# A decoder block on one core: vector work of the latent attention in pieces between products, four GpSimd operations moved to VectorE, stores of x pinned

## The chip, the cores and the metric

The kernel runs on one core of a Trainium2 chip. The metric is the device time of one execution in microseconds (us); of several runs the median counts. The engines of the core are named as in the profile: PE (TensorE, matrix products), DVE (VectorE), ACT (ScalarE), POOL (GpSimd) and SP (SyncE, which here issues nearly all the DMAs). Each engine works through its own queue of instructions in order, and waits for the other engines by semaphores.

## What is computed

Two decoder blocks for 512 tokens of width 1024, all in fp32. The first has four mixers side by side on one projection, then a feed-forward layer. The second has a gated linear recurrence beside a windowed attention, then attention to a memory of 256 tokens, then a convolutional feed-forward layer. Cut to what the change touches:

```
h = rms_norm(x, norm1_w);  cols = split_cols(h @ w_in, IN_SIZES)
y_a = short_conv_mixer(a_b, a_c, a_u, conv_w, conv_b)      # v = a_c * a_u;  a_b * (conv(v) + conv_b)
y_b = nsa_mixer(...)                                       # compressed + selected + windowed attention
y_c = mla_mixer(m_cq, m_ckv, m_kr, ...)                    # latent attention, below
y_d = stick_breaking_mixer(...)
x = x + grouped_rms_norm([y_a, y_b, y_c, y_d]) @ w_out;    x = x + relu(rms_norm(x) @ w1)**2 @ w2

def mla_mixer(c_q, c_kv, k_rope, ...):
    q = rms_norm(c_q) @ wq_b;  kv = rms_norm(c_kv) @ wkv_b       # 4 heads
    q = [q_nope, rope(q_rope)];  k = [k_nope, rope(k_rope)]
    o = causal_attention(rms_norm(q), rms_norm(k), v)

# second block
o = gla(q, 1 - f, log f, v) forward + backward              # 4 heads, 128 wide
y = gate * (rms_norm(o) * silu(g)) @ w_rec + gate * window_attention(...) @ w_att
mem_n = rms_norm(mem);  x = x + softmax((rms_norm(x) @ w_q) @ k_mem) @ v_mem @ w_o
```

## The kernel before

Tokens are cut into four tiles of 128. Every fp32 product is made of three passes: the left and the right operand are each split into a high and a low part (`Hkh`, `Hkl` for the normed input, `whi`, `wlo` for a weight), and PE multiplies high by high (L183), low by high (L184) and high by low (L185). A weight goes by a DMA of SP into `wraw`; ACT writes `whi` from it (L258) and DVE writes `wlo` (L259).

There is no written order of instructions over the whole program. The code is made of generators: a main line calls for attention heads step by step, and a side queue `fq` holds generators of projections. `fill(n)` takes n steps from the side queue, so that the products of projections stand on PE between the small products of an attention, during whose softmax on DVE and ACT PE would otherwise be idle. `drain()` runs what is left of the queue. A scheduler then puts the instructions of each engine into an order, roughly the order of the code, but it may move an instruction ahead of another where nothing forbids it.

In the first block (`side2`, in the function that runs the four mixers) the order is: the projection of the latent attention with `ncv` as its result; eight stores of x to `xs` (L674), from which x is read back later; `mla_stats`, which sums squares on ACT, takes a reciprocal root and scales `ncv` by it; `conv`, the projection of the convolution; the transposes and projections of the latent attention; `mla_rope`, which rotates, sums squares, takes a reciprocal root and scales again; `conv_gate`, the projection of the convolution's gate. `conv` and `conv_gate` yield in the middle of their products, the two others ran at one go. While this stands in the side queue, the heads of the sparse attention (NSA) are on the main line: for each unit of them the logits `L` are made by L889 and L890, DVE masks them and takes their maximum (L827, tiles `sba` and `sbam`), ACT makes the exponential (L828), PE transposes (L833, `pT`), ACT or DVE copy the transposed tile (`sbe`, L837 or L839), and PE multiplies by the values (L844).

`rsqrt_mean` makes a reciprocal root in one of two ways: for twelve or more columns by Ln and Exp on ACT with one step of Newton's method on DVE, for fewer by a power on POOL (L226). `token_rs` calls it with the sum of squares of each token, which L426 makes from `nacc`.

In the second block the recurrence runs over levels (`gla_head`): the product of level 0 needs a sum `gym` that POOL makes (L1549), its result is `lv` (L1555), and each further level needs products of DVE. After each level the main line takes steps of the side queue, which holds the projections of the next heads, of the gate and of `qkv`. The memory's norm (`token_rs` at L1741) stands between products of the cross-attention; its result reaches PE as `pt` (L439).

Of the kernel before, what the change touches and what calls it, by code (L numbers as in the profile page):

```python
# [148 lines left out]
class Kern:  # L149
# [50 lines left out]

    def rsqrt_mean(self, pool, out, ss, inv_n, tag):

        nc = self.nc
        n = 1
        for d in ss.shape[1:]:
            n *= d
        t = self.T(pool, [P] + list(ss.shape[1:]), F32, tag + "t")
        p = ss.shape[0]
        nc.vector.tensor_scalar(t[:p], ss, inv_n, EPS, op0=OP.mult, op1=OP.add)
        if n >= 12:  # L210

            u = self.T(pool, [P] + list(ss.shape[1:]), F32, tag + "u")[:p]
            t = t[:p]
            nc.scalar.activation(u, t, AF.Ln)
            nc.scalar.activation(out, u, AF.Exp, scale=-0.5)
            nc.vector.tensor_mul(u, out, out)
            nc.vector.tensor_mul(u, u, t)
            nc.vector.tensor_scalar(u, u, -0.5, 1.5, op0=OP.mult, op1=OP.add)
            nc.vector.tensor_mul(out, out, u)
            return  # L220
        e = self.mhalf[:p, :n]
        if len(ss.shape) == 3:
            e = e.rearrange("p (a b) -> p a b", b=ss.shape[2])
        elif len(ss.shape) == 4:
            e = e.rearrange("p (a b c) -> p a b c", b=ss.shape[2], c=ss.shape[3])
        nc.gpsimd.tensor_tensor(out, t[:p], e, op=OP.pow)  # L226
# [137 lines left out]
    def weave(a, b, n):  # L364

        for _ in a:
            yield
            for _ in range(n):
                next(b, None)
                yield  # L370

    def drain(self):
        self.fill(1 << 30)
# [45 lines left out]

    def token_rs(self, acc, N, inv_n, tag="o"):  # L420

# [5 lines left out]
        rs = self.T(self.sp, [P, nt], F32, "rs", 4)  # L427
        self.rsqrt_mean(self.sp, rs, stv[:, :, 0], inv_n, "rs")
        return rs
# [121 lines left out]
    def mixers1(self):  # L551
# [41 lines left out]
        with tc.tile_pool(name="mx", bufs=1) as mp:  # L593
# [69 lines left out]
            def side2():  # L663
# [8 lines left out]
                st["g"] = gN.rearrange("p t (h b) -> p t b h", b=3)  # L672
                for k in range(8):
                    nc.sync.dma_start(xs[:, k, :], self.x[k])  # L674
                self.mla_stats(mp, ncv)
                yield from self.conv(mp, nm, w)
                self.group_out(ySB, 3, "pT")
                cq = self.mla_trans(mp, ncv)
                yield
                yield from self.mla_proj(mp, ncv, cq, st)  # L680
                self.mla_rope(mp, ncv, st["mla"])
                yield from self.conv_gate(nm, w, st)
                norm = self.conv_norm(st["acc"])
# [267 lines left out]
    def conv(self, mp, nm, w):  # L951
# [3 lines left out]
        def ev_cu(c, b):  # L955
# [6 lines left out]
            nc.vector.tensor_mul(t, b, nm.R)  # L962
            nc.gpsimd.tensor_mul(v[c], t, v[c])
            cw = self.vec(f"cw{c}")
# [7 lines left out]
    def conv_gate(self, nm, w, out):  # L972
# [3 lines left out]
        def ev_b(c, b):  # L976
            y = self.yT[c]
            t = self.T(self.sp, [P, S], F32, "nsq", 2)
            nc.vector.tensor_mul(t, b, nm.R)
            nc.gpsimd.tensor_mul(y, y, t)  # L980
            self.dbg(f"yA{c}", y)
            if c == 0:
                nc.scalar.activation(acc, y, AF.Square)
            else:
                sq = self.T(self.sp, [P, S], F32, "nsq", 2)
                nc.scalar.activation(sq, y, AF.Square)
                nc.gpsimd.tensor_add(acc, acc, sq)
        yield from self.tproj_g(nm.H, w, [(0, 256)], ev_b)
# [255 lines left out]
    def mla_stats(self, mp, ncv):  # L1244
        nc = self.nc
        ss = self.T(mp, [P, NT, 2], F32, "mss", 1)
        for t in range(NT):
            nc.scalar.activation(self.junk(mp)[:, :192], ncv[:, t, :192], AF.Square, accum_out=ss[:, t, 0:1])
            nc.scalar.activation(self.junk(mp)[:, :128], ncv[:, t, 192:320], AF.Square, accum_out=ss[:, t, 1:2])
        nc.vector.tensor_scalar(ss[:, :, 0:1], ss[:, :, 0:1], 128.0 / 192.0, None, op0=OP.mult)  # L1250
        rr = self.T(mp, [P, NT, 2], F32, "mrr", 1)
        self.rsqrt_mean(mp, rr, ss, 1.0 / 128, "mrr")
        for t in range(NT):
            nc.vector.tensor_scalar(ncv[:, t, 0:192], ncv[:, t, 0:192], rr[:, t, 0:1], None, op0=OP.mult)
            nc.vector.tensor_scalar(ncv[:, t, 192:320], ncv[:, t, 192:320], rr[:, t, 1:2], None, op0=OP.mult)

    def mla_trans(self, mp, ncv):
# [38 lines left out]
    def mla_rope(self, mp, ncv, m):  # L1296
# [11 lines left out]
        for t in range(NT):  # L1308
            rope(qN[t][:, :, 64:96], t, 4)
            kr = ncv[:, t, 320:352].unsqueeze(1)  # L1310
            rope(kr, t, 1)
            nc.gpsimd.tensor_copy(kN[t][:, :, 64:96], kr.to_broadcast([P, 4, 32]))
        ss2 = self.T(mp, [P, 2, NT, 4], F32, "mss2", 1)
        for a, x in enumerate((qN, kN)):
            for t in range(NT):
                sq2 = self.T(mp, [P, S], F32, "mla_p", 3)[:, :384].rearrange("p (h d) -> p h d", d=96)
                nc.scalar.activation(sq2, x[t], AF.Square)
                nc.vector.tensor_reduce(ss2[:, a, t], sq2, axis=AX.X, op=OP.add)
        rr2 = self.T(mp, [P, 2, NT, 4], F32, "mrr2", 1)
        self.rsqrt_mean(mp, rr2, ss2, 1.0 / 96, "mrr2")  # L1320
        for a, x in enumerate((qN, kN)):
            for t in range(NT):
                nc.vector.tensor_mul(x[t], x[t], rr2[:, a, t].unsqueeze(2).to_broadcast([P, 4, 96]))

    def mla_head(self, h, prep):
# [71 lines left out]
    def mixers2(self):  # L1397
# [3 lines left out]
        with tc.tile_pool(name="b2", bufs=1) as bp:  # L1401
# [11 lines left out]
            with tc.tile_pool(name="gla", bufs=1) as gp:  # L1413
# [37 lines left out]
                for h in range(4):  # L1451
                    while st["n"] <= h:
                        self.fill(1)
                    if h == 0:
                        self.fill(5)
                    for lv, _ in enumerate(self.gla_head(gp, h, st, v)):
# [257 lines left out]
    def memory(self):  # L1714
# [4 lines left out]
        with tc.tile_pool(name="mem", bufs=1) as kp:  # L1719
# [3 lines left out]
            def prep():  # L1723
# [16 lines left out]
                yield  # L1740
                mn.rs = self.token_rs(mn.acc, 256, 1.0 / D, "pt")  # L1741
                yield
# [199 lines left out]
```

## Time and profile before

| | |
|---|---|
| time, median of 3 runs | 1625.76 us (1625.58 to 1626.16) |
| the profiled execution's own time | 1626.29 us |
| its span, from the first to the last instruction | 1624.6 us, mean granted clock 0.995 |
| PE busy | 1591.5 us, 98% of the span |
| DVE, ACT, POOL busy | 921.0, 667.0, 174.9 us (57%, 41%, 11%) |
| the chain that ended last | PE 90%, DVE 4%, ACT 2% |

The span is the stretch that the profile covers; what lies around it, 1.7 us, belongs to the time but not to the trace. Busy shares of the engines overlap: the chain's line says which engine's work, wait by wait, ended last.

### The profile page before, as it was taken

What the parts mean: (1) busy time and instruction counts of PE and PEld (TensorE: products, weight loads), DVE (VectorE), ACT (ScalarE), POOL (GpSimd) and SP (SyncE); (2) the same over time, 40 slices, a digit from 0 to 9 for tenths busy, and PEclk for the clock granted to TensorE, in tenths of its full rate; (3) what the DMA queues carried; (4) which work ended last, traced back from release to release, by engine and by line L of the source; (5) the groups of instructions that cost most, each with busy time, mean ns of one, the idle gap of its engine ahead of it and who ended that gap; (6) DMA issues with size and microseconds to landing.
All of it is one profiled execution on the core that took longest, in us unless ns stands there. A gap on an engine that the chain in (4) does not pass through costs nothing.

```text
span 1624.6 us, 20813 instructions
## 1 busy us (share of the span) xinstructions
PE 1591.5 (98%) x8049; PEld 1341.8 (83%) x8049; DVE 921.0 (57%) x1503; ACT 667.0 (41%) x1172; POOL 174.9 (11%) x185
## 2 busy tenths in 40 slices
PE   8999999999999999999999999999999999999998
PEld 6798888788888888878888788888988888888886
DVE  6666885644223434475766565664667556526662
ACT  5675554544123423334333354353544233222332
POOL 0121110200000001121110000330002111001110
PEclk9999999999999999999999999999999999999999
DMA  7242131232322223221222211323332333232331
GB/s 225 67 126 85 33 117 40 66 102 92 101 94 98 97 94 100 88 89 55 73 72 78 65 40 59 115 96 118 126 98 84 99 98 97 94 101 91 101 120 52
DMA packets 108118, 148.15 MB, mean 91 GB/s; under 512 B 7887, under 2 KB 58868, under 8 KB 108020
## 3 DMA queue, kind: packets, MB, share of 16 engines
q1 hardware_dynamic: 107876, 146.72, 28.3%
q8 instruction: 63, 1.03, 0.3%
q14 instruction: 35, 0.29, 0.1%
q10 hardware_dynamic: 144, 0.11, 0.0%
HBM read 142.31 MB, written 4.20 MB: 90 GB/s over the span
## 4 chain that ended last, share of the span: by engine, by line
PE 90%; DVE 4%; ACT 2%; issue 1%; POOL 1%; DMA 1%; SPq 0%; POOLq 0%; DVEq 0%; ACTq 0%
PE mm L183 25%; PE mm L185 25%; PE mm L184 25%; PE o L844 2%; PE lv L1570 2%; PE pT L833 1%; PE o L1613 1%; DVE wlo L259 1%; ACT whi L258 1%; PE L L889 1%; DMA wraw<-w_in_dram 1%; DMA wraw<-w_down_dram 1%; PE o L183 0%; PE o L185 0%; PE L L890 0%
## 5 line engine op out<-in xcount | busy, mean ns | idle before, releaser
L259 DVE TENSOR_TENSOR wlo<-wraw,whi 128x1024 fp32r<-128x1024 f32 (+4 forms) x268 | 319.5, 1194 | 439.2 <-ACT whi L258 434.5
L258 ACT ACTIVATE whi<-wraw 128x1024 fp32r<-128x1024 f32 (+4 forms) x268 | 270.4, 1010 | 536.9 <-PE mm L184 470.2
L417 POOL TENSOR_TENSOR nacc<-nacc,nsq 128x512 f32<-128x512 f32 x24 | 37.3, 1553 | 508.7 <-ACT nsq L415 507.6
L1866 POOL TENSOR_TENSOR fz<-fz,fu 128x512 f32<-128x512 f32 x22 | 37.4, 1698 | 269.6 <-ACT fz L1865 269.6
L461 DVE TENSOR_TENSOR x<-mm,x 128x512 f32<-128x512 f32 x72 | 48.9, 687 | 19.1 <-PE mm L185 18.8
L183 PE MATMUL mm<-H4h,whi 128*128 128x512 f32 x147 | 59.3, 404 | 0.0
L183 PE MATMUL mm<-H0h,whi 128*128 128x512 f32 x139 | 55.8, 402 | 2.9 <-ACT whi L258 2.9
L183 PE MATMUL mm<-H6h,whi 128*128 128x512 f32 x147 | 58.1, 399 | 0.4 <-ACT H6h L194 0.4
L183 PE MATMUL mm<-H7h,whi 128*128 128x512 f32 x147 | 58.3, 397 | 0.0
L185 PE MATMUL mm<-H4h,wlo 128*128 128x512 f32 x147 | 57.6, 392 | 0.7 <-DVE wlo L259 0.7
L183 PE MATMUL mm<-H5h,whi 128*128 128x512 f32 x147 | 58.1, 395 | 0.0
L185 PE MATMUL mm<-H6h,wlo 128*128 128x512 f32 x147 | 57.7, 393 | 0.0
L185 PE MATMUL mm<-H5h,wlo 128*128 128x512 f32 x147 | 57.7, 393 | 0.0
L184 PE MATMUL mm<-H6l,whi 128*128 128x512 f32 x147 | 57.7, 393 | 0.0
L184 PE MATMUL mm<-H5l,whi 128*128 128x512 f32 x147 | 57.4, 391 | 0.0
L184 PE MATMUL mm<-H4l,whi 128*128 128x512 f32 x147 | 57.4, 391 | 0.0
L185 PE MATMUL mm<-H7h,wlo 128*128 128x512 f32 x147 | 57.4, 390 | 0.0
L184 PE MATMUL mm<-H7l,whi 128*128 128x512 f32 x147 | 57.3, 390 | 0.0
L185 PE MATMUL mm<-H2h,wlo 128*128 128x512 f32 x139 | 54.5, 392 | 1.1 <-DVE wlo L259 1.1
L183 PE MATMUL mm<-H3h,whi 128*128 128x512 f32 x139 | 55.4, 399 | 0.0
L183 PE MATMUL mm<-H2h,whi 128*128 128x512 f32 x139 | 55.2, 397 | 0.0
L183 PE MATMUL mm<-H1h,whi 128*128 128x512 f32 x139 | 54.9, 395 | 0.0
(1264 smaller groups left out, 4340.1 us busy)
## 6 DMA issues: line engine op xcount, KB each, us to landing
wraw<-ffn_w_dram SPq DMA_DIRECT2D x64, 512.0 KB, 3.6
wraw<-w_up_dram SPq DMA_DIRECT2D x88, 256.0 KB, 2.8
wraw<-w_in_dram SPq DMA_DIRECT2D x36, 512.0 KB, 3.4
wraw<-w_down_dram SPq DMA_DIRECT2D x22, 512.0 KB, 3.6
wraw<-w_mem_kv_dram SPq DMA_DIRECT2D x16, 512.0 KB, 3.7
wraw<-w_in_dram SPq DMA_DIRECT2D x52, 128.0 KB, 2.3
wraw<-w_in_dram SPq DMA_DIRECT2D x20, 256.0 KB, 2.8
wraw<-cmp_w_dram SPq DMA_DIRECT2D x8, 512.0 KB, 4.0
```

Source lines behind the costliest of these rows:

```text
L183: mm(out, a.hi, b.hi, start=start, stop=False, skip_group_check=skip)
L184: mm(out, a.hi, b.lo, start=False, stop=False, skip_group_check=skip)
L185: mm(out, a.lo, b.hi, start=False, stop=stop, skip_group_check=skip)
L258: nc.scalar.activation(hi, raw, AF.Copy)
L259: nc.vector.tensor_sub(lo, raw, hi.bitcast(F32))
L417: eng.tensor_add(nm.acc, nm.acc, sq[:, :nm.N])
L461: self.nc.vector.tensor_add(self.x[k], b, self.x[k])
L833: nc.tensor.transpose(b[:, t * P:(t + 1) * P], st["p"][:, t * P:(t + 1) * P], self.ident)
L844: nc.tensor.matmul(o(), st["pT"][:, t * P:(t + 1) * P], v(t), start=(t == 0), stop=(t == nt - 1))
L889: self.nc.tensor.matmul(out, q[h][:, qs], k.hi[:, ks], start=True, stop=False)
L1570: nc.tensor.matmul(b[:, t * P:(t + 1) * P], ym[:, t * P:(t + 1) * P], mix(X, c, t * P, P), start=True, stop=True)
L1866: nc.gpsimd.tensor_mul(z, z, us[c])
```

## The change

Seven edits. (1) The stores of x become the last pieces of a generator, pinned to their place in the program, and run along with `conv`. (2) `mla_stats` yields after each tile and runs along with `conv` too, one piece per step. (3) `mla_rope` yields likewise and runs along with `conv_gate`, two pieces per step. (4) The product `v = a_c * a_u` of the convolution (L963) goes from POOL to DVE. (5) So do the product of the gate (L980) and the sum of its squares (L987). (6) Ahead of the first level of the first recurrence head, ten steps of the side queue are taken where there were five. (7) The memory's reciprocal root is made by Ln, Exp and Newton's method, though it has two columns.

```diff
-    def rsqrt_mean(self, pool, out, ss, inv_n, tag):
+    def rsqrt_mean(self, pool, out, ss, inv_n, tag, newton=False):
...
-        if n >= 12:
+        if n >= 12 or newton:
...
+    @staticmethod
+    def along(a, pieces, n=1):
+
+        for _ in a:
+            for _ in range(n):
+                next(pieces, None)
+            yield
+        for _ in pieces:
+            pass
...
-                for k in range(8):
-                    nc.sync.dma_start(xs[:, k, :], self.x[k])
-                self.mla_stats(mp, ncv)
-                yield from self.conv(mp, nm, w)
+
+                def store():
+                    for k in range(8):
+                        tc.keep_in_program_order(nc.sync.dma_start(xs[:, k, :], self.x[k]))
+                        yield
+                yield from self.along(self.conv(mp, nm, w), itertools.chain(self.mla_stats(mp, ncv), store()))
...
-                self.mla_rope(mp, ncv, st["mla"])
-                yield from self.conv_gate(nm, w, st)
+                yield from self.along(self.conv_gate(nm, w, st), self.mla_rope(mp, ncv, st["mla"]), 2)
...
-            nc.gpsimd.tensor_mul(v[c], t, v[c])
+            nc.vector.tensor_mul(v[c], t, v[c])
...
-            nc.gpsimd.tensor_mul(y, y, t)
+            nc.vector.tensor_mul(y, y, t)
...
-                nc.gpsimd.tensor_add(acc, acc, sq)
+                nc.vector.tensor_add(acc, acc, sq)
...
                     if h == 0:
-                        self.fill(5)
+                        self.fill(10)
...
-                mn.rs = self.token_rs(mn.acc, 256, 1.0 / D, "pt")
+                mn.rs = self.token_rs(mn.acc, 256, 1.0 / D, "pt", True)
```

What is left out are the yields within `mla_stats` (after each tile, and after the root) and `mla_rope` (likewise), and the flag that `token_rs` hands on. The changed kernel has twelve lines more near its head and a few after, so its line numbers are higher.

On PE, ahead of the first level of the first recurrence head, the order of before is this (`mm` are projections of the next heads, `lv` the level's product):

```order
L183 MATMUL mm_6083<-H2h_5489,whi_6087 128x512
L184 MATMUL mm_6083<-H2l_5490,whi_6087 128x512
L185 MATMUL mm_6083<-H2h_5489,wlo_6088 128x512
L1555 MATMUL lv_6115<-gq_5944,gym_6112 128x128 x4
L1570 MATMUL lv_6121<-gX_5945,gym_6122 128x128 x4
L183 MATMUL mm_6083<-H3h_5503,whi_6087 128x512
```

At the same place the changed kernel has, behind the three products with H2 that stand above:

```order
L184 MATMUL mm_6083<-H3h_5503,whi_6087 128x512
L185 MATMUL mm_6083<-H3l_5504,whi_6087 128x512
L186 MATMUL mm_6083<-H3h_5503,wlo_6088 128x512
L184 MATMUL mm_6084<-H2h_5489,whi_6087 128x512
L185 MATMUL mm_6084<-H2l_5490,whi_6087 128x512
L186 MATMUL mm_6084<-H2h_5489,wlo_6088 128x512
L184 MATMUL mm_6084<-H3h_5503,whi_6087 128x512
L185 MATMUL mm_6084<-H3l_5504,whi_6087 128x512
L186 MATMUL mm_6084<-H3h_5503,wlo_6088 128x512
L184 MATMUL mm_6085<-H2h_5489,whi_6087 128x512
L185 MATMUL mm_6085<-H2l_5490,whi_6087 128x512
L186 MATMUL mm_6085<-H2h_5489,wlo_6088 128x512
```

Then come `lv` of L1574 and L1589. Twelve products have moved ahead of the level.

On DVE, where the convolution's first tile is made (`cv` is the product a_c * a_u, `yT` the convolution, `nsq` the projection times the norm), before:

```order
L966 TENSOR_SCALAR yT_441_1929<-cv_429_1886,vecs_75 128x512
L968 SCALAR_TENSOR_TENSOR yT_441_1929<-cv_429_1886,vecs_75,yT_441_1929 128x511
L962 TENSOR_TENSOR nsq_1954<-mm_1576,R_328 128x512
L968 SCALAR_TENSOR_TENSOR yT_441_1929<-cv_429_1886,vecs_75,yT_441_1929 128x510
L966 TENSOR_SCALAR yT_448_1957<-cv_432_1902,vecs_75 128x512
L827 ISA sba_1965,sbam_1964<-L_1961,sbLh_1307 128x256
L827 ISA sbam_1964 128x1
L968 SCALAR_TENSOR_TENSOR yT_448_1957<-cv_432_1902,vecs_75,yT_448_1957 128x511
L195 SCALAR_TENSOR_TENSOR mla_t_1993<-mm_1987,vecs_75,mla_p_1992 128x512
```

And in the changed kernel:

```order
L975 TENSOR_TENSOR cv_429_1886<-nsq_1926,cv_429_1886 128x512
L978 TENSOR_SCALAR yT_441_1929<-cv_429_1886,vecs_75 128x512
L980 SCALAR_TENSOR_TENSOR yT_441_1929<-cv_429_1886,vecs_75,yT_441_1929 128x511
L974 TENSOR_TENSOR nsq_1954<-mm_1538,R_328 128x512
L980 SCALAR_TENSOR_TENSOR yT_441_1929<-cv_429_1886,vecs_75,yT_441_1929 128x510
L975 TENSOR_TENSOR cv_432_1902<-nsq_1954,cv_432_1902 128x512
L839 ISA sba_1965,sbam_1964<-L_1961,sbLh_1307 128x256
L839 ISA sbam_1964 128x1
L978 TENSOR_SCALAR yT_448_1957<-cv_432_1902,vecs_75 128x512
L196 SCALAR_TENSOR_TENSOR mla_t_1993<-mm_1987,vecs_75,mla_p_1992 128x512
```

The two products of `cv` now stand on DVE, and the masking of the logits (L827, there L839) has moved ahead of the second tile's L966.

On DVE ahead of the sum of tokens at L426 (`H0l` to `H3l` are the low parts of the queries and keys of the first heads of the latent attention), before:

```order
L979 TENSOR_TENSOR nsq_2526<-mm_2300,R_328 128x512
L1104 TENSOR_TENSOR nlc_2433<-nlc_2433,nsc_2440 128x128
L1138 TENSOR_TENSOR ev_2504<-o_2186,ncf_2501 128x512
L195 SCALAR_TENSOR_TENSOR H0l_2545<-mm_2539,mwq_2209,H0h_2544 96x512
L195 SCALAR_TENSOR_TENSOR H1l_2554<-mm_2548,vecs_75,H1h_2553 96x512
L195 SCALAR_TENSOR_TENSOR H2l_2563<-mm_2557,mwq_2209,H2h_2562 96x512
```

And in the changed kernel:

```order
L991 TENSOR_TENSOR nsq_2526<-mm_2213,R_328 128x512
L210 TENSOR_SCALAR grs1t_2512<-gss_606_2508 128x1
L196 SCALAR_TENSOR_TENSOR H0l_2545<-mm_2539,mwq_2209,H0h_2544 96x512
L801 TENSOR_SCALAR yq_2317<-yq_2317,grs_608_2511 128x256
L992 TENSOR_TENSOR yT_448_1957<-yT_448_1957,nsq_2526 128x512
L196 SCALAR_TENSOR_TENSOR H1l_2554<-mm_2548,vecs_75,H1h_2553 96x512
L196 SCALAR_TENSOR_TENSOR H2l_2563<-mm_2557,mwq_2209,H2h_2562 96x512
L999 TENSOR_TENSOR nacc_2211<-nacc_2211,nsq_2529 128x512
```

The gate's second product (L992) and the sum `nacc` (L999) are now in DVE's queue, behind the low parts of the heads; before, both were on POOL.

## Rows read from the trace of the kernel before

**Rows 1.** The page's busy time: us, share of the span, instructions.

```profile
PE 1591.5 (98%) x8049; PEld 1341.8 (83%) x8049; DVE 921.0 (57%) x1503; ACT 667.0 (41%) x1172; POOL 174.9 (11%) x185
```

**Rows 2.** Waits of PE: what ended them, total us, times, longest us.

```profile
PE lv L1555 <- POOL gym L1549: 2.2, 1, 2.2
...
PE pt L439 <- DVE nsq L437: 1.6, 1, 1.6
PE pT L833 <- DVE sbe L839: 1.5, 2, 1.2
...
PE pT L1114 <- DVE sbe L839: 1.2, 1, 1.2
...
PE L L1090 <- DVE sbam L827: 0.9, 1, 0.9
```

**Rows 3.** Windows: length; busy us of PE, PEld, DVE, ACT, POOL; clock; DMA.

```profile
177.93:181.33 3.40, 3.40 (x10) 2.73 (x10) 2.88 (x6) 0.60 (x1) 0.00 (x0) 0.50 0.03 7
707.00:710.40 3.40, 3.40 (x17) 3.30 (x16) 2.04 (x3) 1.17 (x2) 0.00 (x0) 0.50 0.45 148
...
188.00:214.00 26.00, 24.79 (x150) 20.92 (x149) 24.57 (x87) 17.01 (x43) 5.21 (x8) 1.00 0.22 71
```

**Rows 4.** Timeline of SP: start, us, engine, line, operation, tiles, count.

```profile
16.68 0.94 SPq L674 DMA_DIRECT2D xs<-x  x2
```

**Rows 5.** Timeline of DVE near the start; in brackets idle time and its releaser.

```profile
34.62 0.17 DVE L754 CAST rpf<-rpi 128x4 f32<-128x4 int32 x1 [0.44 <-DMA rpi<-positions_dram]
35.27 0.29 DVE L517 CAST cmatr<-R 128x256 fp32r<-128x256 f32 x1 [0.48 <-DMA R<-cmat_dram]
```

**Rows 6.** Timeline of PE near the start.

```profile
42.98 0.50 PE L183 MATMUL mm<-whi,H2h 128*128 128x512 f32 x1 [1.45 <-ACT whi L258]
```

**Rows 7.** Timeline of DVE, the first scaling of `mla_stats`.

```profile
142.62 0.32 DVE L1254 TENSOR_SCALAR ncv<-ncv,mrr 128x192 f32<-128x192 f32 x1 [1.40 <-POOL mrr L226]
```

**Rows 8.** Timeline of DVE in the convolution.

```profile
171.47 0.55 DVE L966 TENSOR_SCALAR yT<-cv,vecs 128x512 f32<-128x512 f32 x1 [0.90 <-POOL cv L963]
...
172.72 0.68 DVE L962 TENSOR_TENSOR nsq<-mm,R 128x512 f32<-128x512 f32 x1
...
175.23 0.55 DVE L966 TENSOR_SCALAR yT<-cv,vecs 128x512 f32<-128x512 f32 x1 [1.17 <-POOL cv L963]
175.69 0.42 DVE L827 CUSTOM_DVE_ANT_0 sba<-L,sbLh 128x256 f32<-128x256 f32 x1
...
178.91 0.75 DVE L195 SCALAR_TENSOR_TENSOR mla_t<-mm,vecs,mla_p 128x512 fp32r<-128x512 f32 x1
```

**Rows 9.** Timeline of PE, the product with the third `mla_t`.

```profile
180.99 0.56 PE L185 MATMUL mm<-whi,mla_t 128*128 128x512 f32 x1
```

**Rows 10.** Timeline of PE at the sum of tokens of the convolution.

```profile
221.02 1.05 PE L426 MATMUL mm<-ones,nacc 128*128 128x2 f32 x8 [1.43 <-POOL nacc L987]
```

**Rows 11.** Timeline of DVE ahead of it.

```profile
218.92 0.74 DVE L195 SCALAR_TENSOR_TENSOR H2l<-mm,mwq,H2h 96x512 fp32r<-96x512 f32 x1
```

**Rows 12.** Timeline of PE ahead of the first level of the recurrence.

```profile
703.68 0.39 PE L184 MATMUL mm<-H2l,whi 128*128 128x512 f32 x1
703.91 0.39 PE L185 MATMUL mm<-H2h,wlo 128*128 128x512 f32 x1
706.52 1.67 PE L1555 MATMUL lv<-gq,gym 128*128 128x128 f32 x8 [2.23 <-POOL gym L1549]
```

**Rows 13.** Timeline of POOL there.

```profile
704.75 1.72 POOL L1549 TENSOR_TENSOR gym<-gY 128x512 f32<-128x512 f32 x1
```

**Rows 14.** Timeline of POOL at the memory's reciprocal root.

```profile
1081.66 0.70 POOL L226 TENSOR_TENSOR rs<-rst,mhalf 128x2 f32<-128x2 f32 x1 [4.40 <-DVE rst L209]
```

**Rows 15.** The table load at line 1531, ahead of the recurrence: ns min/median/max, first and last start.

```profile
L1531 ACT ACT_TABLE_LOAD  x1: 1283/1283/1283, 696.1 to 696.1; - x1
```

**Rows 16.** Timeline of ACT behind the memory's reciprocal root.

```profile
1084.13 1.06 ACT L258 ACTIVATE whi<-wraw 128x1024 fp32r<-128x1024 f32 x1 [4.16 <-issue]
```

**Rows 17.** Timeline of DVE, the memory's diagonal tiles.

```profile
1090.22 1.49 DVE L437 TENSOR_SCALAR nsq<-cmat,rs 128x128 f32<-128x128 f32 x2
```

More of the change, by code (lines that the diff above doesn't have):

```diff
@@ L1 @@
+import itertools
 import math
@@ L418, in norm_tile, with token_rs @@
         nm.k += 1
-    def token_rs(self, acc, N, inv_n, tag="o"):
+    def token_rs(self, acc, N, inv_n, tag="o", newton=False):
         nt = N // P
@@ L427, in token_rs @@
         rs = self.T(self.sp, [P, nt], F32, "rs", 4)
-        self.rsqrt_mean(self.sp, rs, stv[:, :, 0], inv_n, "rs")
+        self.rsqrt_mean(self.sp, rs, stv[:, :, 0], inv_n, "rs", newton)
         return rs
@@ L1249, in mla_stats @@
             nc.scalar.activation(self.junk(mp)[:, :128], ncv[:, t, 192:320], AF.Square, accum_out=ss[:, t, 1:2])
+            yield
         nc.vector.tensor_scalar(ss[:, :, 0:1], ss[:, :, 0:1], 128.0 / 192.0, None, op0=OP.mult)
@@ L1252, in mla_stats @@
         self.rsqrt_mean(mp, rr, ss, 1.0 / 128, "mrr")
+        yield
         for t in range(NT):
@@ L1255, in mla_stats @@
             nc.vector.tensor_scalar(ncv[:, t, 192:320], ncv[:, t, 192:320], rr[:, t, 1:2], None, op0=OP.mult)
+            yield
     def mla_trans(self, mp, ncv):
@@ L1312, in mla_rope @@
             nc.gpsimd.tensor_copy(kN[t][:, :, 64:96], kr.to_broadcast([P, 4, 32]))
+            yield
         ss2 = self.T(mp, [P, 2, NT, 4], F32, "mss2", 1)
@@ L1318, in mla_rope @@
                 nc.vector.tensor_reduce(ss2[:, a, t], sq2, axis=AX.X, op=OP.add)
+                yield
         rr2 = self.T(mp, [P, 2, NT, 4], F32, "mrr2", 1)
         self.rsqrt_mean(mp, rr2, ss2, 1.0 / 96, "mrr2")
+        yield
         for a, x in enumerate((qN, kN)):
@@ L1323, in mla_rope @@
                 nc.vector.tensor_mul(x[t], x[t], rr2[:, a, t].unsqueeze(2).to_broadcast([P, 4, 96]))
+                yield
     def mla_head(self, h, prep):
```

## Prediction

> **What bounds the kernel now.** I read the busy table first. TensorE (PE) is busy 98% of the span of 1624.6 us [rows 1], so time can only be saved where PE stands idle or runs slowly. The list of PE's waits comes second: of its single waits those that this change touches are small, 0.9 to 2.2 us each [rows 2]. The reader is to see that no wait returns in a loop: each happens once, at one place of the program, and so each must be answered for by itself. Third come windows with the granted clock. In two stretches of 3.4 us the clock is 0.50, its lower level of 1.2 GHz, while PE is busy all through [rows 3]. Such a stretch does 1.7 us of full-speed work, so it costs 1.7 us. Four of them lie in the trace away from its two ends, each shortly behind idle time of PE: the one at 177.93 follows the wait of 0.9 at L1090, and the one at 707.00 follows the wait of 2.2 at `lv`. Not every wait has one behind it (the 1.6 at `pt` and the 1.2 at L1114 have none). A wait that goes may therefore be worth its own length or 1.7 us more.
>
> The second thing to see is VectorE (DVE). Over the whole span it is far from full, but from 188 to 214 it is busy 24.57 of 26 us [rows 3]. Work that is moved to DVE there is not free.
>
> **The start.** The eight stores of `xs` go out of the first weight loads on the queue of SP, two of which take 0.94 us to issue [rows 4]. What stood behind them comes earlier: DVE had waited 0.44 us for the positions and 0.48 us for `R` [rows 5], 0.92 together, and behind these came the copies on ScalarE (ACT), the next `whi`, and PE's wait of 1.45 us [rows 6]. I take 0.9; the ends are 0 (if another load is now the late one) and 1.45. Where the stores land now, seven ahead of conv's fourth weight load, they cost 7 x 0.47 = 3.3 us of SP's time; I cost them at nothing, because the third load's products run meanwhile. Without that cover PE would wait up to those 3.3 us.
>
> **`mla_stats` in pieces.** Before, DVE waited 1.40 us for GpSimd's (POOL) power and then did eight scalings, with the copy `sbe` queued behind them [rows 7]; PE's wait for that copy is 1.2 [rows 2]. The copy now goes ahead. But the power starts later, since the last sum of squares on ACT stands behind more of the softmax, and the next logits (L827) are queued behind three scalings that wait for it; the copy that PE wants next hangs on these. So the stall is moved one unit on: I take 0, with ends of a gain of 1.2 and a loss of 0.7 (the wait of 1.40 shared by half with PE).
>
> **The convolution's product on DVE.** Before, DVE waited 0.90 and 1.17 us for POOL's two products. L827, for which PE waits 0.9 us at L1090, was issued at 175.69 [rows 2, 8]. Now the products are on DVE, at 0.68 each, as its own product of that shape (`nsq`) shows. The waits of 2.07 go, 2 x 0.68 = 1.36 come, and L966 (0.55) falls behind L827: 175.69 - 2.07 + 1.36 - 0.55 = 174.4. PE gets to L1090 at 176.17 - 0.88 = 175.3, so this wait goes, and I take it that the half-clock stretch behind it goes too: 0.9 + 1.7 = 2.6. What is late next is the third `mla_t`: DVE ended it at 178.91 + 0.75 = 179.66, and now 0.7 sooner, at 178.95. PE used it at 180.99 [rows 9]; with 0.9 less of waiting and 1.5 less of slow clock by then, it wants it at 178.5. A wait of 0.5 is left: 2.1, say 2.0. The ends are 0.4, if the slow stretch stays, and 2.6.
>
> **Rope and gate.** Rope, squares and scalings of the latent attention are spread through the products of `conv_gate`, so that `wlo`, L827 and `sbe` stand ahead of them on DVE; the wait of 1.2 at L1114 [rows 2] should go. PE is then 1.2 us sooner at L426, where it already waited 1.43 us for POOL's `nacc` [rows 10]. That sum is now on DVE, behind H1l and H2l. Before, H2l ended at 218.92 + 0.74 = 219.7 [rows 11]. If idle time of DVE takes up all the rest, `nacc` ends at 219.7 + 0.7 = 220.4; if none does, the two products of the gate (1.36) and two small pieces (0.5) come on top, 222.2. In a window that is 94% full I take the middle, 221.3, against 221.0 before. The 1.2 is thus turned into a longer wait at L426, and the two edits together give -0.3, with ends of -1.2 and +0.6; were the slow stretch behind L426 to go too, 1.7 more.
>
> **`fill(10)` ahead of the first recurrence head.** PE does 12 products more before the first `lv`. They start 0.227 us apart (703.68 and 703.91, and so on through the run), 12 x 0.227 = 2.7 us; PE would have reached `lv` at 706.52 - 2.23 = 704.3 and now does at 707.0 [rows 12]. POOL ends the sum for which it waits at 704.75 + 1.72 = 706.5 [rows 13]. So the whole 2.23 goes, with 0.5 to spare, and the slow stretch with it: 2.2 + 1.7 = 3.9. The order shows that each later gap between the levels has as many products as before or more, and that 15 are missing at the end of the recurrence, where they stand between small transposes: 15 x 0.227 = 3.4 us if all of that cover is needed. In each of those places only three to five of about twenty are gone, so I take 0 and keep 3.4 as the end.
>
> **The memory's reciprocal root.** POOL's power (0.70 us from 1081.66) is replaced by Ln and Exp on ACT, each with a table load of 1.283 us, and four small operations on DVE [rows 14, 15]. ACT is idle for 4.16 us up to 1084.13 [rows 16], and so the chain can be done at about 1081.6 + 0.2 + 1.3 + 0.2 = 1083.3 on ACT if the first load runs ahead of its data, at 1084.6 if not; the root is wanted by DVE only at 1090.22 [rows 17]. PE's wait of 1.6 at `pt` follows from that DVE operation (1.49 us for two that run beside POOL) and stays. I take 0; if the next `whi` is pushed, up to 0.5 is lost. A load before the memory's softmax goes; nothing waited for it.
>
> The Trainium skill, on its page "ScalarE: Activation LUTs" (What ACT_TABLE_LOAD costs), speaks against this edit: it puts a switch of table set at 1283 ns for the load and some 1380 ns of drain behind it. By it, an estimate, two switches would end at about 1085.7, past the start of `whi`, and the sum would be 1.6 us less. This trace agrees on the load, 1283 ns; no row of it shows a drain.
>
> **The sum.** 0.9 + 0 + 2.0 - 0.3 + 3.9 + 0 = 6.5 us. Against the profiled execution's own 1626.29 (1624.6 of span and 1.7 around it) that gives 1619.8; the median of the runs shown is 0.53 lower, and so I predict 1619.3.
>
> **Rivals.** First, DVE in the attention gives back what the waits gave: the start gives 0, the pieces of `mla_stats` lose 0.7, the convolution gains 0.4, the gate loses 1.2. That is -1.5, with the recurrence's 3.9 a gain of 2.4, 1623.4. For it speaks the window that is 94% full; against it, that 2.07 us of waits for POOL leave DVE's queue.
>
> Second, the slow stretches stay where they are, since they don't follow every wait and so may hang on more than that one: 6.5 - 3.4 = 3.1, 1622.7. Against it: both stretches here stand right behind the waits that go.
>
> Third, a switch of ACT's table costs more than its load. With each of the two taking as long again (a second 1.283, from the row of the load), the chain ends at 1083.3 + 2.6 = 1085.9, `whi` and everything on DVE behind it is 1.8 us late, and PE's wait at `pt` grows by as much, with a slow stretch of 1.7 behind it at worst: 6.5 - 3.5 = 3.0, 1622.8. That is the rule of the page "ScalarE: Activation LUTs" of the Trainium skill, named above. The rows show an idle ACT there, and no drain.
>
> Fourth, and slower: DVE becomes the bound from 188 to 224. The 2.04 us added there (three operations of 0.68) sit ahead of the logits of each unit, and PE meets the delay not once but at every unit: at three units 3 x 2.0 = 6.1 of waiting, with a slow stretch of 1.7 behind two of them 9.5. Set against 0.9 + 2.0 + 3.9 = 6.8, it is slower by 2.7 before the -0.3 of the gate: 1625.8 + 3.0 = 1628.8. It decides from about 6.8 + 3.3 = 10 us of new waits and slow stretches. Against it: such a lag is paid once, unless DVE keeps falling behind.
>
> **Chances.** The forecast 0.55, first rival 0.15, second 0.10, third 0.08, fourth 0.12. I call a change of more than 0.2% (3.3 us) different from none, about what a measurement of this kernel can tell: below 1622.5 is faster. The forecast holds 1616 to 1622.4; the first three rivals straddle the line, and I give 0.09 of their 0.33 to faster, the rest to same. With a little of the forecast's spread taken off, faster 0.62, same 0.27, slower 0.11. All terms at their better ends give 11 us less, 1614.5; the fourth rival's upper part is left out: 1615 to 1626.
>
> **What would show it.** Right: no PE wait for POOL at `lv`, and a clock of 1.00 behind it; L1090 without a wait, and no slow stretch at 178; at L426 a wait of some 2.5 to 3 us, now for DVE; the wait at `pt` still about 1.6; the first `whi` of 42.98 about 0.9 sooner. Wrong: new waits of PE for `sbam` or `sbe` between 188 and 224, a half-clock stretch in the recurrence, a `pt` wait that grows, or waits at the transposes that end the recurrence.

## The result and the profile after

The changed kernel takes 1616.84 us (median of 6 runs, 1616.16 to 1617.34) against 1625.67 for the kernel before (6 runs, 1623.94 to 1626.16): the ratio is 0.9947, with an interval of 0.9937 to 0.9958. That is 8.8 us less, 0.54%. The forecast was 1619.3, faster, in a range of 1615 to 1626; the sign and the range held, and the gain was 2.3 us larger than the sum.

The profiled execution of the changed kernel has a span of 1614.9 us, 9.7 less than the one shown of before. Its busy times answer to [rows 1]:

```profile
PE 1587.4 (98%) x8049; PEld 1340.4 (83%) x8049; DVE 920.7 (57%) x1512; ACT 669.8 (41%) x1175; POOL 167.0 (10%) x179
```

POOL has six operations fewer: five of the three lines that moved to DVE (two for each product, one for the sum) and the power of the memory's root. PE does the same 8049 products. It is busy 4.1 us less, in part because two half-clock stretches are gone, and the rest of the 9.7 is idle time that went. The list of PE's waits (columns as in [rows 2]) shows which: the waits for `gym`, for `sbam` at L1090, for `sbe` at L1114 are no longer in it.

```profile
PE mm L437 <- DVE nacc L999: 2.6, 1, 2.6
PE pt L450 <- DVE nsq L448: 1.5, 1, 1.5
PE lv L1589 <- DVE gX L1618: 1.2, 1, 1.2
...
PE mm L186 <- DVE mla_t L196: 0.4, 1, 0.4
```

Where the 9.7 us lie is best read from equal instructions of PE in both traces, by how much sooner each starts after:

| PE's instruction | before | after | sooner by | gained in the stage |
|---|---|---|---|---|
| first product of 128x512 | 9.82 | 8.76 | 1.06 | 1.06 |
| product with H2h and the first late `whi` | 42.98 | 41.09 | 1.89 | 0.83 |
| transpose of `nlc`, behind `mla_stats` | 146.87 | 143.93 | 2.94 | 1.05 |
| third `mla_t`, behind the convolution | 180.99 | 175.97 | 5.02 | 2.08 |
| product with H6h, behind the attention's output | 283.60 | 278.65 | 4.95 | -0.07 |
| `pt`, behind the recurrence, the window and the mix | 1091.86 | 1082.20 | 9.66 | 4.71 |
| end of the span | 1624.6 | 1614.9 | 9.7 | 0.0 |

The windows of the changed kernel (columns as in [rows 3]) show the clock at the convolution, behind L437, and at the recurrence's first level:

```profile
171.00:177.00 6.00, 5.60 (x38) 4.63 (x37) 5.93 (x12) 3.23 (x9) 0.00 (x0) 1.00 0.01 1
217.94:221.35 3.41, 3.41 (x19) 3.28 (x18) 2.72 (x6) 2.85 (x5) 0.77 (x1) 0.50 0.38 106
...
700.00:703.40 3.40, 3.40 (x22) 3.05 (x21) 3.37 (x4) 0.48 (x2) 1.58 (x1) 1.00 0.18 70
```

The two stretches that the forecast said would go are gone, and the two that it left are there, at 217.94 and at 279.38. At the recurrence PE's timeline reads, against [rows 12]:

```profile
701.93 1.06 PE L1574 MATMUL lv<-gq,gym 128*128 128x128 f32 x8
```

and POOL's, against [rows 13]:

```profile
699.84 1.74 POOL L1568 TENSOR_TENSOR gym<-gY 128x512 f32<-128x512 f32 x1
```

The sum ends at 701.58 and PE comes at 701.93: 0.35 us to spare, no bracket, no wait.

### The profile page after: what moved, and what is told of

It is laid out like the page before. It is cut to its first block, busy times and chain, and to the rows that moved or that the text cites. A ratio compares the mean times of both kernels' runs of the same rounds, so it can differ in the third digit from the quotient of the medians.

```text
span 1614.9 us, 20830 instructions
## 1 busy us (share of the span) xinstructions
PE 1587.4 (98%) x8049; PEld 1340.4 (83%) x8049; DVE 920.7 (57%) x1512; ACT 669.8 (41%) x1175; POOL 167.0 (10%) x179
## 4 chain that ended last, share of the span: by engine, by line
PE 94%; DVE 3%; ACT 2%; issue 1%; POOL 0%; DMA 0%; SPq 0%; POOLq 0%; DVEq 0%; ACTq 0%
PE mm L184 26%; PE mm L186 26%; PE mm L185 26%; PE o L856 2%; PE lv L1589 2%; PE pT L845 1%; PE o L1632 1%; DVE wlo L260 1%; PE L L901 1%; ACT whi L259 1%; PE L L902 1%; PE o L184 0%; PE o L186 0%; PE o L185 0%; PE o L958 0%
## 5 line engine op out<-in xcount | busy, mean ns | idle before, releaser
L185 PE MATMUL mm<-H0l,whi 128*128 128x512 f32 x139 | 54.9, 395 | 0.0
```

Of the source, the lines that this page charges most:

```text
L185: mm(out, a.hi, b.lo, start=False, stop=False, skip_group_check=skip)
```

## The experiments

Twelve kernels were run. Times are medians; the kernel before, run beside them on the same chips, had 1625.36, 1625.65 and 1625.42 in the three groups.

**1. The recurrence's fill alone.**

```diff
                     if h == 0:
-                        self.fill(5)
+                        self.fill(10)
```

> The kernel before with ten steps of the side queue ahead of the first recurrence head, nothing else. My theory: PE's wait of 2.23 us at lv goes, and the half-clock stretch of 3.4 us behind it (1.7 us) goes with it, 3.9 us; with what the change as a whole showed in the recurrence (about 4.7 us between the first level and the memory) 3.9 to 4.7 us, so 1621.0 to 1621.8 against 1625.7. Rival: the slow stretch is not caused by this wait and only 2.2 us come, 1623.5, with a clock of 0.50 still found near 707.

Measured: 1621.53 (8 runs), ratio 0.9976 (0.9966 to 0.9986): 3.8 us less. From the product of 397 us, behind the attention stage, to `pt` PE gains 4.86 us in its trace, as in the full change (4.7). The wait at `lv` is gone and the clock is 1.00 from 224.8 to the last microseconds. This edit alone is worth 3.8 to 4.9 us. That the stretch went because the wait went is not shown: experiment 5 has the same wait and no stretch.

**2. Seven steps instead of ten.**

```diff
# against the changed kernel
-                        self.fill(10)
+                        self.fill(7)
```

> The changed kernel with seven steps there instead of ten: three products of 0.227 us stand ahead of the level in addition to those of before, where ten steps gave twelve. PE's wait at lv should be 2.23 - 0.68 = 1.55 us. If the slow stretch goes with the length of the wait, none follows, as none follows the wait of 1.5 at pt in the memory stage: 1616.8 + 1.6 = 1618.4. Rival: any wait at this place brings the slow stretch, whose 1.7 us come back too: 1620.1.

Measured: 1621.20 (8 runs), ratio 0.9974 (0.9964 to 0.9985). PE's timeline has the wait as worked out, 1.55:

```profile
701.37 0.82 PE L1574 MATMUL lv<-gq,gym 128*128 128x128 f32 x5 [1.55 <-POOL gym L1568]
```

No half-clock stretch follows it in this trace (701.37 to 704.77 has a clock of 1.00). So the rival's claim that any wait here brings the stretch falls, and yet the time is nearer the rival's: 4.4 us above the changed kernel where 1.6 was expected. All of PE's idle time in the recurrence is 5.4 us, against 2.7 with ten steps. Besides the 1.55, PE meets new waits further on, 0.83 for ACT's `gym` at the level of 725 and 0.43 for a `wlo` at 754. Nine products fewer than with ten steps stand ahead of the first level, but ahead of the level of 725 there are 15, as with ten steps; so the number of products in that gap is not the cause, and what is, no run shows. The idle time accounts for 2.8 of the 3.8 us that the stage loses in the trace; the last 1.0 I can't assign.

**3. The convolution's product alone.**

```diff
-            nc.gpsimd.tensor_mul(v[c], t, v[c])
+            nc.vector.tensor_mul(v[c], t, v[c])
```

> The kernel before with the convolution's product (L963) on DVE, nothing else. My theory: the wait of 0.9 us at L1090 and the slow stretch behind it go, a wait of about 0.5 for the third mla_t comes: a gain of 2.0, 1623.7. The rope of the latent attention is still in one piece on DVE behind it, so the wait at L1114 and the wait for nacc stay as they were. Rival: DVE only carries the two products later, the gain is passed on to the wait at L1114 or at L426 (POOL ends nacc no sooner), and the time is within 0.5 us of before.

Measured: 1623.40 (11 runs), ratio 0.9989 (0.9980 to 0.9998): 2.0 us less. PE gains 2.2 us between the transpose of `nlc` and the third `mla_t`, waits 0.39 there, and keeps all of it (1.93 sooner at the product of 397 us, 1.91 at the end). The rival falls. From the transpose to the third `mla_t` it takes 32.0 us, the kernel before 34.1, and experiments 5 and 6, which have the wait of 0.9 at the logits but no half-clock stretch behind it, take 32.9. So of the 2.2 us some 1.0 are the waits and 1.2 the stretch, and that the stretch hangs on the wait is not shown.

**4. The gate's three operations back on POOL.**

```diff
# against the changed kernel
-            nc.vector.tensor_mul(y, y, t)
+            nc.gpsimd.tensor_mul(y, y, t)
...
-                nc.vector.tensor_add(acc, acc, sq)
+                nc.gpsimd.tensor_add(acc, acc, sq)
```

> The changed kernel with the gate's product and the sum of squares back on POOL. My theory says that the wait of 2.56 us at the sum of tokens is made by DVE's queue, in which the sum stands behind the low parts of two heads. On POOL the same three operations take 1.28 + 1.28 + 1.26 us against 3 x 0.68, but don't queue behind DVE: I expect nacc 0 to 1 us sooner than in the changed kernel and the time at 1616.0 to 1617.0. Rival: POOL stands behind yq and its own products, nacc comes later than now, and the time is 0.5 to 2 us longer than 1616.8, which would make the move of these operations worth that much.

Measured: 1614.67 (5 runs, 1614.40 to 1616.59), ratio 0.9937 (0.9924 to 0.9949): less than the changed kernel by 1.6 us if the two ratios are compared (0.0010 of 1625), by 2.2 if the medians are. The intervals of the two ratios overlap. But the four kernels that are made from the changed one and have the gate's products back on POOL (experiments 4, 8, 10 and 12) have medians of 1613.8 to 1615.5, and those with the products on DVE (the changed kernel and experiment 9) 1616.8 and 1618.6. So this part of the change made it slower. PE's timeline:

```profile
215.78 0.38 PE L437 MATMUL mm<-ones,nacc 128*128 128x2 f32 x2 [1.99 <-POOL nacc L999]
```

The wait is 1.99 instead of 2.56, the changed kernel's wait of 0.68 at 212 is gone too, and no half-clock stretch follows. Of the 2.6 us that its trace gains on the changed kernel's from the late `whi` to `pt`, 1.1 are these waits; 1.4 come at the two places where the changed kernel has a stretch and this one has none.

**5. The stores alone.**

```diff
-                for k in range(8):
-                    nc.sync.dma_start(xs[:, k, :], self.x[k])
                 self.mla_stats(mp, ncv)
-                yield from self.conv(mp, nm, w)
+                def store():
+                    for k in range(8):
+                        tc.keep_in_program_order(nc.sync.dma_start(xs[:, k, :], self.x[k]))
+                        yield
+                yield from self.along(self.conv(mp, nm, w), store())
```

> The kernel before with the eight stores of x pinned and spread through conv, nothing else. My theory: the 0.92 us that DVE waited for the positions and for R near 35 us go, and PE's wait of 1.45 us at 42.98 falls to about 0.5, as in the changed kernel: a gain of 0.9. The changed kernel showed 1.9 there; the other 1.0 lay ahead of the first product at 8.8 us and I take it for the chance of when the first pieces of x land, so it shouldn't belong to this edit. Rival: the stores also held back the very first loads, and this kernel too is 1.9 us sooner at its product of 43 us.

Measured: 1623.98 (10 runs), ratio 0.9991 (0.9982 to 1.0001), some 1.5 us less, not clear of none. The wait at the late `whi` is 0.52 as in the changed kernel, where the five other kernels with the old stores have 1.16 to 1.49. The product of 43 us is 1.25 us sooner than in the trace of before: PE is 0.32 sooner up to that product, and 0.93 come at it (in the changed kernel 0.96 and 0.93). Kernels with the same stores reach it at 40.85 to 43.41: the first products start at 8.76 to 10.50, and that differs from run to run. So 0.9 belongs to the edit, and the rest of the 1.9 shown after I put down to chance.

This trace shows one thing more. PE waits 0.9 us at the logits (L1102 here, L1090 before) and 2.2 at `lv`, as in the kernel before:

```profile
704.87 1.16 PE L1567 MATMUL lv<-gq,gym 128*128 128x128 f32 x8 [2.22 <-POOL gym L1561]
```

Yet the clock behind both waits is 1.00. From `lv` to the same product eight microseconds on, PE takes 7.18 us here and 8.38 in the kernel before, where the stretch is: the stretch cost 1.2 us, not 1.7. Near 284 us, where this trace again has no stretch, it cost 0.5: without it PE is idle for 0.6 us there.

**6. `mla_stats` in pieces alone** (its yields, and `along(self.conv(...), self.mla_stats(...))`, with the stores as before).

> The kernel before with mla_stats in pieces along conv, nothing else (the stores go as before). My prediction had 0 for this edit, since the next logits would queue behind the scalings; in the changed kernel PE was 1.0 us sooner by 147 us than the start accounts for, and the wait of 1.2 us for sbe was gone. New theory: that 1.0 belongs to this edit alone, offset at the transposes of nlc -1.0 against its own start. Rival: it came from the freed loads of the stores, and the wait moves to another place here, offset 0.

Measured: 1624.19 (10 runs), ratio 0.9992 (0.9983 to 1.0001). Against its own start (43.62) the transpose of `nlc` is 1.01 us sooner than before; the wait of 1.2 is gone and no other takes its place, neither here nor later (2.2 sooner against its start at 283 us, 1.2 of which comes with a half-clock stretch at 178 that is not in this trace). By the time alone the gain is not clear of none; by the trace the new theory holds.

**7. The rope in pieces alone** (its yields, and `along(self.conv_gate(...), self.mla_rope(...), 2)`).

> The kernel before with mla_rope in pieces along conv_gate, nothing else; gate product and sum of squares are still on POOL. My theory: the wait of 1.15 us at L1114 goes, and PE meets a longer wait at the sum of tokens (L426), where it waits for POOL: 1.43 + about 1.1 = 2.5 us less what DVE feeds POOL sooner; gain 0 to 0.6 us. Rival: with the rope out of the way DVE gives POOL its inputs sooner by as much, nacc comes 1 us sooner too, and the gain of 1.1 us stays.

Measured: 1624.02 (10 runs), ratio 0.9990 (0.9981 to 0.9999), 1.6 us less. The wait at L1114 is gone, and PE waits 1.99 us at the sum of tokens instead of 1.43. It starts that sum 0.76 us sooner than before, against its own start. That is between the two: of 1.15 us about 0.7 stays.

**8. The memory stage's sums of squares on DVE**, on top of experiment 4.

```diff
-            eng = nc.vector if nm.k == 7 else nc.gpsimd
+            eng = nc.vector if nm.k == 7 or getattr(nm, "dve", 99) <= nm.k else nc.gpsimd
...
             nm = self.nm4 = self.norm_begin(self.hp, "nmem")
+            nm.dve = 4
```

> The changed kernel with the gate's product and sum of squares back on POOL, as in the run before, and with the sums of squares of tiles 4 to 6 of the norm ahead of the memory attention on DVE instead of POOL. PE's wait of 1.5 us at pt is for two operations of DVE that take 1.49 us while POOL adds, where two of that kind take 0.3 each with POOL idle, and the operation ahead of them takes 1.19 instead of 0.75. If POOL's sums slow them, they take 0.5 and 0.75 now; two sums of 0.68 come into DVE's queue ahead of them, and the wait falls from 1.5 to about 0.9: 1614.1 against 1614.7. Rival: the slow operations are not POOL's doing, they stay at 1.5, the sums come on top and the wait grows to 2.5 or more: 1615.7.

Measured: 1615.48 (4 runs: 1613.60, 1613.78, 1617.18, 1617.52), ratio 0.9940 (0.9925 to 0.9955). The time can't tell it from experiment 4, but the traces can. DVE's timeline in experiment 4, where POOL adds:

```profile
1077.43 1.19 DVE L196 SCALAR_TENSOR_TENSOR H5l<-x,vecs,H5h 128x512 fp32r<-128x512 f32 x1
1078.54 1.48 DVE L448 TENSOR_SCALAR nsq<-cmat,rs 128x128 f32<-128x128 f32 x2
```

POOL's timeline there:

```profile
1076.73 3.02 POOL L428 TENSOR_TENSOR nacc<-nacc,nsq 128x512 f32<-128x512 f32 x2 [11.14 <-ACT nsq L426]
```

And DVE's timeline in this experiment, with the sums on DVE:

```profile
1077.63 0.74 DVE L196 SCALAR_TENSOR_TENSOR H5l<-x,vecs,H5h 128x512 fp32r<-128x512 f32 x1
1078.30 0.68 DVE L428 TENSOR_TENSOR nacc<-nacc,nsq 128x512 f32<-128x512 f32 x1
1078.90 0.48 DVE L448 TENSOR_SCALAR nsq<-cmat,rs 128x128 f32<-128x128 f32 x2
```

The same operations take 0.74 and 0.48 instead of 1.19 and 1.48. PE's wait at `pt` was to fall to 0.9 and is gone from the list; `pt` is 0.65 us sooner, the span's end 0.9. The rival falls: beside POOL's sums DVE's operations were longer by 0.45 and 1.0 us. The Trainium skill says on its page "SBUF — State Buffer" (SBUF: two separate sides) that DVE, for an operation in a mode that uses two ports or with two inputs in SBUF, and GpSimd share a pair of ports that one locks for a whole instruction while the other is blocked. These rows agree in that DVE is held up while POOL adds; that it is the ports, and for a whole instruction, they do not show.

**9 and 10. One of the gate's parts back on POOL**, the sum alone and the products alone, to find which of them is late.

> The changed kernel with the sum of squares (L999) back on POOL and the gate's two products left on DVE. New theory on the wait at the sum of tokens: DVE isn't full there, it stands idle for 1.48 us at grs1t, which waits for ACT, and the second product of the gate, whose input is ready at 211.1, is queued behind that and starts at 213.69. By it this kernel gains nothing: the product is as late, ACT's square ends at 215.0, POOL's sum of 1.27 ends at 216.3, where DVE's ended at 216.3; the wait at L437 stays at about 2.5 us. Rival (as my prediction had it): the sum behind H1l and H2l on a full DVE makes the wait, and it falls by 0.6 or more here.

Measured: 1618.64 (4 runs), ratio 0.9958 (0.9941 to 0.9974). That is 1.8 us above the changed kernel; its trace is already 1.3 later at the late `whi`, and 0.9 more come behind it. PE's timeline has a wait as long as with the sum on DVE:

```profile
217.74 0.49 PE L437 MATMUL mm<-ones,nacc 128*128 128x2 f32 x3 [2.65 <-POOL nacc L999]
```

> The changed kernel with the gate's two products back on POOL and the sum of squares left on DVE. By the new theory this one gains: the second product starts at about 211.8 on POOL, as in the kernel with both back on POOL, ends at 213.1, and the sum is at DVE's turn behind H2l at about 215.0 at the latest: the wait at L437 falls from 2.56 to 1.3 to 2.0 us, and the time by 0.6 to 1.2 us, and by up to 1.7 more when no half-clock stretch follows. Rival: the sum's place behind the low parts makes the wait, and it stays at 2.5.

Measured: 1614.82 (4 runs), ratio 0.9937 (0.9922 to 0.9952). PE's timeline:

```profile
215.43 0.72 PE L437 MATMUL mm<-ones,nacc 128*128 128x2 f32 x5 [1.36 <-DVE nacc L999]
```

The products made the wait, not the sum; the rival falls in both. With the products on POOL the sum is even better off on DVE: the wait is 1.36, against 1.99 with both on POOL. The timeline of DVE in the changed kernel shows how:

```profile
210.45 0.68 DVE L991 TENSOR_TENSOR nsq<-mm,R 128x512 f32<-128x512 f32 x1
212.61 0.15 DVE L210 TENSOR_SCALAR grs1t<-gss 128x1 f32<-128x1 f32 x1 [1.48 <-ACT junk L797]
212.68 0.74 DVE L196 SCALAR_TENSOR_TENSOR H0l<-mm,mwq,H0h 96x512 fp32r<-96x512 f32 x1
...
213.69 0.69 DVE L992 TENSOR_TENSOR yT<-yT,nsq 128x512 f32<-128x512 f32 x1
...
215.61 0.68 DVE L999 TENSOR_TENSOR nacc<-nacc,nsq 128x512 f32<-128x512 f32 x1
```

The product's input is there at 211.13. Ahead of the product stands an operation on one column that waits 1.48 us for ACT, while DVE is idle; behind that come the low part of a head (0.74) and a scaling (0.35). So the product, for which PE waits, starts at 213.69, 2.56 us after its input is there. On POOL (experiment 10) it starts at 212.08.

**11. The memory's root alone** (the last argument of `token_rs`).

> The kernel before with the memory's reciprocal root by Ln, Exp and Newton's method, nothing else. My theory: no change, since ACT is idle for 4.16 us there and DVE wants the root only 8 us later; the wait at pt stays at 1.5 to 1.6 us, and the span from the first product of 397 us to the end is that of before within 0.3 us. Rival (the drain behind a table load that a page of notes states): the next whi of ACT starts 1.6 us later, and the wait at pt grows.

Measured: 1627.06 (10 runs), ratio 1.0010 (1.0001 to 1.0019): slower by 1.6 us. ACT's timeline shows the chain:

```profile
1080.68 1.28 ACT L214 ACT_TABLE_LOAD   x1
1082.31 0.20 ACT L214 ACTIVATE rsu<-rst 128x2 f32<-128x2 f32 x1 [0.34 <-DVE rst L209]
1082.53 1.28 ACT L215 ACT_TABLE_LOAD   x1
1083.83 0.20 ACT L215 ACTIVATE rs<-rsu 128x2 f32<-128x2 f32 x1
```

The first load runs ahead of its data, as taken; 0.02 us lie between Ln and the second load, and 0.02 between that and Exp. The next `whi` starts at 1084.78 and waits 0.75 for PE, not for the chain. The wait at `pt` is 1.51. Here no drain is seen behind a load, and the measurement decides against the figure for it that the Trainium skill gives on "ScalarE: Activation LUTs" (What ACT_TABLE_LOAD costs); the load's 1283 ns agree. From the product of 397 us to the end this trace loses 0.2 us, so as far as one trace shows, the 1.6 us are not in this stage. The trace has the same four half-clock stretches as the one of before and ends 0.8 us later, and 0.7 of that is there by 20 us, in code that the two kernels share. The mean granted clock of its 10 runs averages 0.9953, that of the 13 runs of the kernel before beside them 0.9965. But at one and the same clock, 0.995, seven of its runs take 1627.2 us on average and 19 of the kernel before 1626.2, so the stretches can be no more than a part of it. The cause stays open, and as no run takes this edit out of the changed kernel, so does what it costs there.

**12. A better version**: experiment 8, and the sum of tokens one head later.

```diff
-                    if h % 2:
+                    if h >= 2:
                         next(norm, None)
```

> The changed kernel with the gate's operations back on POOL, the memory stage's sums of squares on DVE, and the convolution's sum of tokens taken one head later (after the third head of the latent attention instead of the second). PE then has eight transposes more, about 1.0 us, ahead of it: the wait at the sum of tokens falls from 1.99 to about 1.0 us. The broadcast of the root follows one head sooner behind it than before, so up to 0.5 us could come back there. I expect 0.5 to 1.0 us less than the kernel without the last step, 1613 to 1614 where no half-clock stretch falls. Rival: the wait only moves to the broadcast, and nothing is gained.

Measured: 1613.77 (4 runs, 1613.55 to 1615.05), ratio 0.9929 (0.9915 to 0.9944): the lowest median of all, 3 us below the changed kernel, but not clear of experiments 4, 8 and 10, whose intervals overlap with it. PE starts the sum at 218.02 after a wait of 1.08, as expected, now for DVE's `H3l`; no new wait at the broadcast. So the wait is shorter by 0.9; that the last step makes the kernel faster is not shown by the time.

## Why the prediction was right, point by point

The sum was 6.5 us, the medians lie 8.8 apart and the two traces 9.7. Of the 9.7, 1.0 is chance at the start; `mla_stats` and the recurrence gave 1.0 and 0.8 more than was said. Two terms came out near their forecast with parts that did not.

**The start: right, 0.9.** The late `whi` costs PE 0.52 instead of 1.45 in every kernel with the new stores. The 1.06 us at the first product are there before the first edited instruction runs; they go with the start, which differs from run to run.

**`mla_stats`: mis-sized, 0 where it gained 1.0.** The step that failed is "the stall is moved one unit on". It was right that the next logits stand behind three scalings that wait for POOL, and DVE waits there even longer, 1.53 us. But PE did not stop for it: its wait at the next transpose was 0.22. Experiment 6 shows that the 1.0 belongs to this edit.

**The convolution's product: right in sum, its parts not.** 2.1 us in the full change, 2.2 alone, for 2.0; the wait left for the third `mla_t` is 0.40 for the 0.5 forecast. DVE ends that tile sooner by the way that was worked out: its two products took the place of 2.07 us of waiting. But the term took the stretch at 1.7 and the waits at 0.4 net; by experiments 3, 5 and 6 it was 1.2 and 1.0, and the stretch can be absent with the wait in place. That the sum agrees to 0.1 is luck in part.

**Rope and gate: right in size, wrong in cause.** Forecast -0.3, measured -0.07, and the wait at the sum of tokens is 2.56 where 2.5 to 3 was said. But the reason given, a DVE that is full and a sum that stands behind the low parts of two heads, is not what the runs show: experiment 9 moved that sum away and nothing changed. It was the second product, behind a small operation that waited for ACT on an idle DVE and 1.1 us of work behind that. That the wait came out at the 2.5 to 3 that was said is luck. The prediction's "if idle time of DVE takes up the rest" and "if none does" both missed that idle time can stand in front of an operation instead of taking it up. Without the gate's move the rope would have given about 0.7 (experiment 7) and the whole change 1.6 to 2.2 more (experiment 4).

**The recurrence: right on the wait, mis-sized at 3.9 for 4.7.** PE's idle time from the first level to the window fell by 2.2 (4.85 to 2.66), as forecast, and the half-clock stretch went. But the stretch was worth 1.2 and not 1.7 (experiment 5), and the 2.2 agree by luck: the wait of 1.05 for a `wlo` near 761 went too, which the forecast did not have, and as much came back. At the last transposes 0.4 came (0.53 to 0.92), of the end of 3.4 for missing cover. At a level 0.9 came (0.30 to 1.22), and that is not missing cover, as 15 products stand ahead of it before and after: a `wlo` of 0.68 us that DVE made behind `gX` before (at 826.76) now stands ahead of it (at 818.48), and PE waits for `gX`. The other 1.3 lies in PE's busy time, not in waits: from the product of 703 us to 1000 us before, and from the same product at 698.07 to 990.20 after, 1674 operations keep PE busy for 291.8 and 289.3 us, and 1.2 of that difference is the stretch. Their order differs; which of them take less stays open.

**The memory's root: right at its place, 0.** The wait at `pt` is unchanged because it was never the root's; POOL's sums beside DVE made it (experiment 8), as the prediction noted without using it. That the edit alone measures 1.6 us slower was not foreseen, and why is open.

**The rivals.** The first and the fourth (DVE gives it back, or becomes the bound) came true in one place only, for 2 us. The second fell in its time, since both stretches went; its doubt that a stretch hangs on the wait ahead of it was right (experiment 5). The third fell with experiment 11 as far as its mechanism goes: the next `whi` did not wait for the chain, and the wait at `pt` did not grow.

## What to carry to other kernels

Before work is moved from GpSimd to VectorE, look at what stands ahead of it in VectorE's order, not at how full the engine is: here a faster engine (0.69 for 1.27 us) delivered later, because it stood in the queue behind a small operation that waited for another engine. Where an operation of VectorE takes several times its usual length, look for an operation of GpSimd beside it; taking that away removed a wait of 1.5 us that none of the seven edits touched. A wait at the start of a stage can be filled with work put ahead of it, but that work is taken from a later place, and what comes with it (here the making of a weight's low part) moves too: look at both places.

## What was not expected of the chip

The half-clock stretches of 3.41 us don't follow from the wait in front of them. At the same sum of tokens a wait of 1.42 or 1.43 us had one behind it in six traces (the kernel before, experiments 1, 3, 5, 6 and 11; in 5 it lasted twice as long, 6.83), a wait of 1.99 had none in three (experiments 4, 7 and 8), and 2.56 or 2.65 had one in three (the changed kernel, experiments 2 and 9). Behind the same small waits of 0.37 and 0.42 us near 280 us the changed kernel has one, experiment 4 has none. The two waits that the forecast tied to a stretch, 0.9 at the logits and 2.2 at `lv`, had none behind them in experiment 5, and the first had none in experiment 6. They also differ between executions of one kernel: of the 59 runs of the kernel before in the three groups, 19 had a mean clock of 0.995 and took 1626.2 us on average, 26 had 0.997 and took 1624.9. Nor does a stretch cost half its length: where traces with and without it can be compared over the same products, it cost 1.2 us at two places and 0.5 at a third. A gain that is worked out from the stretches of one profiled execution is therefore only likely, and a difference of one or two microseconds need not come from the code that was changed (experiment 11).
